# A state-space layer's gelu and its split issued per chunk inside the chunk loop, with the two scratch sets exchanging slots

## The chip, the cores and the metric

One core of one Trainium2 chip runs the whole program. The metric is the device time of one execution in microseconds (us), median of three runs. The engines are TensorE (PE, matmuls; its weight loads are PEld), VectorE (DVE), ScalarE (ACT), GpSimd (POOL) and SyncE (SP, which issues the DMAs). Each works through its own queue in order and waits on semaphores.

## The reference, cut to what matters

The network has two blocks in float32 over 256 tokens and 1024 channels. The first block runs four layers (short convolution, S5 state space, RWKV-7, short convolution), each ended by a gated projection and a layer norm. The second block runs over tokens and a context. The change sits in the state-space layer:

```python
u, z = jnp.split(x @ w_in, 2, axis=-1)
...
states = lax.associative_scan(_ssm_combine, (a_seq, bu), axis=1)[1]
y = jnp.einsum("blgp,ghp->blgh", states, c_mat).real + d_skip.astype(f32).reshape(SSM_GROUPS, SSM_GROUP) * ug
y = jax.nn.gelu(y.reshape(bsz, seqlen, D_INNER).astype(x.dtype))
y = y * jax.nn.sigmoid(y @ w_glu + b_glu)
return (y * jax.nn.silu(z)) @ w_out
```

## The kernel before

Activations lie as 8 chunks of 128 channels by 256 tokens. A large matmul takes three passes: weight and activation are each split into a rounded part (`hi`) and the rest (`lo`), and hi·hi, hi·lo and lo·hi are summed. So a 1024x128 weight tile is 24 matmuls of 128x256, and costs one DMA (L605), one ACT copy (`whi`, L606) and one DVE subtraction (`wlo`, L607), issued up to four tiles ahead. `split` does the same to an activation: an ACT copy and a DVE subtraction.

The state-space layer (`ssm`, L968) runs its 8 chunks through the generator `group(c)`, two at a time (`par`). A chunk computes cosines and sines of its angles (`phases`: two sines on ACT, which need ACT's sine table), projects (PE into `ps_ca`, `ps_cb`; ACT copies to `w`), rotates (DVE multiplies and adds, 128x1024 and 128x512), scans (8 DVE scans), rotates back, multiplies by C on PE (`ps_st`) and adds the skip (DVE, writes `y[:, c]`). Its scratch is one of two sets of two slots, `ssm_m`: the even chunks' set lies in slots 6 and 7, the odd chunks' in slots 0 and 1. A slot is a fixed place; a new tile in it waits until the last reader of the old one is done. `ys`, the split gelu, is made in slots 0 and 1, the odd set's.

After the loop, for all 8 chunks: gelu on ACT, then the split. Then the GLU matmul (8 tiles, 192 matmuls), whose results go through tanh on ACT and two products on DVE into `g` (split again), and the output matmul over `g`.

Two more things share the engines. A *context* stream (the second block's context, its first feed-forward: `squares`, `tc`, `h`, `td`, `d`) begins when `ssm` sets its stage after the chunk loop; from then on a planner (`weave`) alternates the two streams in program order by modelled times, taking the context's steps where the first block's stream is modelled as waiting, and a scheduler orders each engine's queue from that program. And a side chain (`junk`, L1384, with 512 KB loads from `in_ada`) is dealt out in between, except while the chunk loop holds it back.

Of the kernel before, what the change touches and what calls it, by code (L numbers as in the profile page):

```python
# [13 lines left out]
AF = mybir.ActivationFunctionType  # L14
# [6 lines left out]
NCH = D // 128  # L21
# [3 lines left out]
RAW = ("ssm_in",)  # L25
# [417 lines left out]
class Net:  # L443
# [491 lines left out]
    def phases(self, c, q_, make):  # L935


        A, V = self.A, self.V
        tsh, _, rho, f2 = self.pre[:4]
        if q_ not in self.sets:  # L940
            self.sets[q_] = tuple(self.slot(k, [2048], f"ssm_m{k}") for k in ((6, 7), (0, 1))[q_])
        a, b = self.sets[q_]
        m1, m2, w = (t.rearrange("p (i q t) -> p i q t", i=4, q=2) for t in (a[:, :1024], a[:, 1024:], b[:, :1024]))
        co, si = (b[:, 1024 + 512 * k:1536 + 512 * k].rearrange("p (i t) -> p i t", i=4) for k in range(2))
        v, kk = (a[:, 1024 + 512 * k:1536 + 512 * k].rearrange("p (i t) -> p i t", i=4) for k in range(2))
        if make:
            for i in range(4):
                self.tc.keep_in_program_order(A.activation(out=v[:, i], in_=tsh, func=AF.Identity, scale=f2[:, 4 * c + i:4 * c + i + 1]))
            A.activation(out=kk, in_=v, func=AF.Identity, bias=self.fixed[MAGIC])
            V.scalar_tensor_tensor(out=v, in0=kk, scalar=MAGIC, in1=v, op0=ALU.subtract, op1=ALU.subtract)  # L950
            self.act(si, v, AF.Sin, scale=-TWO_PI)
            A.activation(out=v, in_=v, func=AF.Abs)
            self.act(co, v, AF.Sin, scale=-TWO_PI, bias=self.fixed[1.5707963])
        return m1, m2, w, co, si
# [7 lines left out]
    def ssm(self, X):  # L962
        nc = self.nc
        x, xs = X
        V, A, T = self.V, self.A, self.T
        N = S // 2
        tt = lambda o, a, b, op: V.tensor_tensor(out=o, in0=a, in1=b, op=op)
        MUL, ADD, SUB = ALU.mult, ALU.add, ALU.subtract  # L968
        tsh, t11, rho, f2, bT, gm, ca, cm = self.pre
        full = lambda i, n: self.slot(i, [NCH, S], n)  # L970
        u, sz = full(8, "u"), full(9, "sz")

        def take(m, ps):
            if m < NCH:
                A.activation(out=u[:, m], in_=ps, func=AF.Copy)
            else:
                self.act(sz[:, m - NCH], ps, AF.Silu)


        came = []  # L980

        def project():
            for t in tiles:
                yield from self.linear("ssm_in", xs or x, take, tiles=(t,))
                came.append(t)

        tiles = [0, 1, 2, 3] + [t for c in range(4) for t in (NCH + c, 4 + c)] + [NCH + c for c in range(4, 8)]

        y = full(10, "y")
        cn = self.slot(3, [2, 32, 32], "cn")
        for r, cc in ((0, ca), (1, cm)):
            A.activation(out=cn[:, r], in_=cc[:, 1], func=AF.Copy, scale=-1.0)
        free = list(range(2))
        halves = lambda t: t.rearrange("p (t r) -> p r t", r=2)
        two = lambda t: t.rearrange("p (q t) -> p q t", q=2)
        lanes = [slice(32 * i, 32 * i + 32) for i in range(4)]

        def group(c):  # L1000
            q_ = free.pop(0)
            m1, m2, w, co, si = self.phases(c, q_, c > 1)
            while c not in came:
                yield Until(self.now() + 0.3)
            uc = two(self.tmp("ta"))
            A.activation(out=uc, in_=halves(u[:, c]), func=AF.Copy)
            both = lambda t: t.unsqueeze(2).to_broadcast([128, t.shape[1], 2, N])
            yield 2.0
            ps = [self.ps(("ca", "cb")[i % 2])[:, :S] for i in range(4)]
            for q in range(2):  # L1010
                for r in range(2):
                    for i, l in enumerate(lanes):
                        T.matmul(two(ps[i])[:, q], lhsT=bT[1 - r][l, q, c], rhs=uc[l, r], start=r == 0, stop=r == 1, share=4)
            for i in range(4):
                A.activation(out=w[:, i], in_=two(ps[i]), func=AF.Copy)
            tt(m1, w, both(co), MUL)
            tt(m2, w, both(si), MUL)
            tt(w[:, :, 0], m1[:, :, 0], m2[:, :, 1], ADD)
            tt(w[:, :, 1], m2[:, :, 0], m1[:, :, 1], SUB)
            for i in range(4):  # L1020
                for q in range(2):
                    x_ = w[:, i, q]
                    V.tensor_tensor_scan(out=x_, data0=rho[:, 4 * c + i:4 * c + i + 1].to_broadcast([128, N]), data1=x_, initial=0.0, op0=MUL, op1=ADD)
            tt(m1, w, both(co), MUL)
            tt(m2, w, both(si), MUL)
            yield 4.0
            yp = two(self.ps("st")[:, :S])
            for i in range(4):
                T.matmul(yp[lanes[i], 0], lhsT=gm[:, c, lanes[i]], rhs=uc[:, 0], start=True, stop=False, share=4)
            for r, cc in ((0, ca), (1, cm)):  # L1030
                n = N - 1 + r
                for k in range(4):
                    for i in range(4):
                        j = 4 * c + i
                        l_, m_ = ((cc[:, 0, j], m1[:, i, 0]), (cc[:, 0, j], m2[:, i, 1]), (cc[:, 1, j], m2[:, i, 0]), (cn[:, r, j], m1[:, i, 1]))[k]
                        T.matmul(yp[lanes[i], r, N - n:], lhsT=l_, rhs=m_[:, :n], start=r == 1 and k == 0, stop=k == 3, share=4)
            free.append(q_)
            V.scalar_tensor_tensor(out=halves(y[:, c]), in0=halves(u[:, c]), scalar=self.p("ssm_d", c), in1=yp, op0=MUL, op1=ADD)

        self.fine = FINE & 1  # L1040
        self.hold += 1
        yield from self.par((group(c) for c in range(NCH)), 2, project())
        self.fine = False
        self.hold -= 1
        self.stage = "ssm"
        yield 1.0
        raw = "ssm_glu" in RAW
        ys = y if raw else self.pair(0, 1, "ys")
        for c in range(NCH):
            self.tc.keep_in_program_order(self.act(y[:, c], y[:, c], AF.Gelu_apprx_tanh))  # L1050
            if not raw:
                self.split(y[:, c], ys[0][:, c], ys[1][:, c])
        yield 4.0
        g = self.operand("ssm_out", (2, 3), "g")
        hb = self.few.tile([128, NCH], F32, name="hb")
        V.tensor_scalar(out=hb, in0=self.p("b_glu", n=NCH), scalar1=0.5, scalar2=None, op0=MUL)

        def take_g(m, ps):
            th = self.tmp("ta")
            self.act(th, ps, AF.Tanh, scale=0.5, bias=hb[:, m:m + 1])  # L1060
            V.scalar_tensor_tensor(out=th, in0=th, scalar=1.0, in1=y[:, m], op0=ADD, op1=MUL)
            self.put(g, m, th, lambda o: V.scalar_tensor_tensor(out=o, in0=th, scalar=0.5, in1=sz[:, m], op0=MUL, op1=MUL))

        yield from self.linear("ssm_glu", ys, take_g)
        yield 1.5
        return (yield from self.finish(x, g, "ssm_out", "ple_gate1"))

# [906 lines left out]
```

## Time and profile before

| | us |
|---|---|
| median of 3 runs | 2878.42 (2876.4 to 2881.57) |
| profiled execution | 2878.2 |
| its span, first to last instruction | 2876.3 |
| PE busy in it | 2738.9 (95%) |
| DVE, ACT busy | 2130.2 (74%), 1596.7 (56%) |

The profiled execution is 0.2 us from the median and spends 1.9 us outside its span. PE is busy nearly throughout, so the places to look at are the few stretches in which it is not.

### The profile page before, as it was taken

The numbers are of one execution on the slowest core, as the hardware profiler recorded it, in microseconds if no ns is written. First come the engines' busy times: TensorE is split into PE (matmuls) and PEld (weight loads), VectorE is DVE, ScalarE is ACT, GpSimd is POOL, SyncE is SP. The second block draws the span as 40 slices with busy tenths as digits, with TensorE's granted clock in tenths as the row PEclk, the third lists the DMA queues.
The fourth block names the chain that finished last, engine by engine and source line by source line (L and its number), as shares of the span: only waits on it lengthen the run. The fifth ranks groups of instructions, "written<-read, shape, count | busy, mean of one in ns | idle before, by whom it ended". The sixth has DMA issues, their size and how long they took to land.

```text
span 2876.3 us, 58509 instructions
## 1 busy us (share of the span) xinstructions
PE 2738.9 (95%) x23798; PEld 2587.5 (90%) x23798; DVE 2130.2 (74%) x3951; ACT 1596.7 (56%) x2946; POOL 13.0 (0%) x40
## 2 busy tenths in 40 slices
PE   8978799899999999999999999999999999999999
PEld 8967699778998998998999968999999999996999
DVE  8867777666688788898889887777854556676654
ACT  6455555866655465877666766545422234466443
POOL 0000000000000000000000000000000000000000
PEclk9989799999999999999999999999999999999999
DMA  7743355201486665666575644666544433322554
GB/s 273 244 158 111 107 169 176 82 17 41 159 263 226 221 200 176 211 215 202 182 231 186 201 134 150 209 219 208 176 140 133 132 112 109 94 91 62 160 183 140
DMA packets 132749, 467.51 MB, mean 163 GB/s; under 512 B 14720, under 2 KB 19072, under 8 KB 131840
## 3 DMA queue, kind: packets, MB, share of 16 engines
q1 hardware_dynamic: 132480, 463.78, 50.3%
q8 instruction: 187, 3.06, 0.4%
q14 instruction: 82, 0.67, 0.1%
HBM read 462.67 MB, written 1.05 MB: 161 GB/s over the span
## 4 chain that ended last, share of the span: by engine, by line
PE 68%; DVE 13%; DMA 9%; ACT 6%; issue 4%; SPq 0%; DVEq 0%; ACTq 0%
PE ps_mm L436 58%; DMA w<-in_ada_dram 6%; PE ps_ca L436 5%; DVE wlo L607 4%; PE ps_cb L436 2%; DVE junk L1384 2%; ACT whi L606 2%; DVE ssm_m L406 2%; PE ps_st L436 2%; DVE tc L406 1%; PE ps_cb L440 1%; DMA w<-in_ab_in_dram 1%; ACT rw_b L406 1%; ACT L406 1%; DMA w<-in_ffn_in_dram 1%
## 5 line engine op out<-in xcount | busy, mean ns | idle before, releaser
L606 ACT ACTIVATE whi<-w 128x1024 fp32r<-128x1024 f32 (+1 forms) x687 | 716.0, 1043 | 738.1 <-PE ps_mm L436 476.0
L607 DVE TENSOR_TENSOR wlo<-w,whi 128x1024 fp32r<-128x1024 f32 (+1 forms) x687 | 826.0, 1204 | 249.7 <-ACT whi L606 247.0
L436 PE MATMUL ps_mm<-h_hi,whi 128*128 128x256 f32 x3024 | 871.4, 290 | 16.8 <-ACT h_hi L406 12.9
L436 PE MATMUL ps_mm<-h_hi,wlo 128*128 128x256 f32 x3024 | 857.8, 285 | 6.0 <-DVE wlo L607 5.8
L436 PE MATMUL ps_mm<-h_lo,whi 128*128 128x256 f32 x3024 | 855.7, 284 | 1.1 <-DVE h_lo L406 1.0
L436 PEld LDWEIGHTS ps_mm<-h_hi,whi 128*128 128x128 f32 x3024 | 571.9, 190 | 27.2 <-ACT h_hi L406 16.4
L436 PEld LDWEIGHTS ps_mm<-h_lo,whi 128*128 128x128 f32 x3024 | 575.2, 190 | 6.0 <-DVE h_lo L406 2.8
L436 PEld LDWEIGHTS ps_mm<-h_hi,wlo 128*128 128x128 f32 x3024 | 572.8, 190 | 8.5 <-DVE wlo L607 7.8
L1384 DVE SCALAR_TENSOR_TENSOR junk<-w,cond 128x1024 bf16<-128x1024 f32 x288 | 351.7, 1221 | 149.9 <-DMA w<-in_ada_dram 148.8
L436 PE MATMUL ps_mm<-d_hi,whi 128*128 128x256 f32 x1232 | 355.5, 289 | 3.6 <-DVE ctx L406 2.7
L436 PE MATMUL ps_mm<-d_hi,wlo 128*128 128x256 f32 x1232 | 349.6, 284 | 0.6 <-DVE wlo L607 0.6
L436 PE MATMUL ps_mm<-d_lo,whi 128*128 128x256 f32 x1232 | 349.6, 284 | 0.4 <-DVE d_lo L406 0.4
L436 PEld LDWEIGHTS ps_mm<-d_hi,whi 128*128 128x128 f32 x1232 | 232.1, 188 | 8.0 <-issue 5.4
L436 PEld LDWEIGHTS ps_mm<-d_lo,whi 128*128 128x128 f32 x1232 | 233.3, 189 | 3.4 <-issue 1.2
L436 PEld LDWEIGHTS ps_mm<-d_hi,wlo 128*128 128x128 f32 x1232 | 232.6, 189 | 1.6 <-DVE wlo L607 0.8
L406 DVE TENSOR_TENSOR td<-td,ps_mm 128x256 f32<-128x256 f32 x154 | 64.4, 418 | 71.8 <-PE ps_mm L436 70.6
L406 ACT ACTIVATE d_hi<-td 128x256 fp32r<-128x256 f32 x154 | 63.1, 410 | 90.5 <-DVE td L406 89.7
L406 ACT ACT_TABLE_LOAD x80 | 102.6, 1283 | 2.1 <-PEq L1965 0.7
L436 PE MATMUL ps_mm<-x_hi,whi 128*128 128x256 f32 x256 | 73.9, 289 | 10.7 <-ACT whi L606 10.7
L406 ACT ACTIVATE tc<-tc 128x256 f32<-128x256 f32 x182 | 75.0, 412 | 5.2 <-DVE tc L406 2.4
L436 PE MATMUL ps_mm<-xs_hi,whi 128*128 128x256 f32 x256 | 73.3, 287 | 4.8 <-ACT xs_hi L406 4.6
L406 ACT ACTIVATE td<-ps_mm 128x256 f32<-128x256 f32 x154 | 57.4, 374 | 32.7 <-PE ps_mm L436 32.2
(466 smaller groups left out, 5233.8 us busy)
## 6 DMA issues: line engine op xcount, KB each, us to landing
w<-in_ffn_in_dram SPq DMA_DIRECT2D x268, 512.0 KB, 4.0
w<-in_ada_dram SPq DMA_DIRECT2D x168, 512.0 KB, 4.3
w<-in_ffn_out_dram SPq DMA_DIRECT2D x96, 512.0 KB, 4.0
w<-in_conv_in_dram SPq DMA_DIRECT2D x64, 512.0 KB, 4.7
w<-in_ffn_out_dram SPq DMA_DIRECT2D x48, 384.0 KB, 3.1
w<-in_ab_in_dram SPq DMA_DIRECT2D x34, 512.0 KB, 4.2
w<-in_ple_gate_dram SPq DMA_DIRECT2D x32, 512.0 KB, 4.3
w<-in_conv_out_dram SPq DMA_DIRECT2D x16, 512.0 KB, 4.8
```

What stands on the lines that cost most here:

```text
L406: return f(**kw)
L436: self.t.matmul(out, lhsT=lhsT, rhs=rhs, start=start, stop=stop)
L440: self.t.transpose(out, in_, ident)
L606: nc.scalar.activation(out=hi[:, :n], in_=w[:, :n], func=AF.Copy)
L607: nc.vector.tensor_tensor(out=lo[:, :n], in0=w[:, :n], in1=hi[:, :n].bitcast(F32), op=ALU.subtract)
L1384: nc.vector.scalar_tensor_tensor(out=self.junk, in0=w, scalar=1.0, in1=cb[:, s], op0=ALU.mult, op1=ALU.mult, accum_out=m[:, t, s:s + 1])
```

## The change

`gelu` and `split` of a chunk move into `group`, behind the line that writes `y[:, c]`. Nothing is issued for the first six chunks; when the seventh is summed, `ys` is made and all seven are done in one go, and the eighth follows when it is summed. The two scratch sets exchange slots: the even chunks now use slots 0 and 1, which `ys` takes over, so it waits for chunk 6 and no more for chunk 7. The loop behind the chunk loop goes.

```diff
-            self.sets[q_] = tuple(self.slot(k, [2048], f"ssm_m{k}") for k in ((6, 7), (0, 1))[q_])
+            self.sets[q_] = tuple(self.slot(k, [2048], f"ssm_m{k}") for k in ((0, 1), (6, 7))[q_])
...
         free = list(range(2))
+        summed, gated, ys = [], set(), []
...
             V.scalar_tensor_tensor(out=halves(y[:, c]), in0=halves(u[:, c]), scalar=self.p("ssm_d", c), in1=yp, op0=MUL, op1=ADD)
+            summed.append(c)
+
+            if len(summed) >= NCH - 1:
+                if not ys:
+                    ys.extend(self.pair(0, 1, "ys"))
+                for k in [k for k in summed if k not in gated]:
+                    gated.add(k)
+                    self.tc.keep_in_program_order(self.act(y[:, k], y[:, k], AF.Gelu_apprx_tanh))
+                    self.split(y[:, k], ys[0][:, k], ys[1][:, k])
...
-        raw = "ssm_glu" in RAW
-        ys = y if raw else self.pair(0, 1, "ys")
-        for c in range(NCH):
-            self.tc.keep_in_program_order(self.act(y[:, c], y[:, c], AF.Gelu_apprx_tanh))
-            if not raw:
-                self.split(y[:, c], ys[0][:, c], ys[1][:, c])
-        yield 4.0
+        yield 1.5
...
-        yield from self.linear("ssm_glu", ys, take_g)
+        yield from self.linear("ssm_glu", tuple(ys), take_g)
```

The orders of the engines show what moves. On ACT, at the end of the chunk loop, before (`sz` is the last silu of the layer, `td` the context's silu; `ACT_TABLE_LOAD` switches ACT's function table):

```order
L406 ACTIVATE sz<-ps_mm 128x256
L406 ACTIVATE squares<-ctx 128x256 x8
L397 ACT_TABLE_LOAD
L406 ACTIVATE tc<-ps_mm,fixed_66 128x256
L406 ACTIVATE tc<-tc 128x256 x2
L406 ACTIVATE h_hi<-tc,mod 128x256 x8
L406 ACT_TABLE_LOAD
L406 ACTIVATE y<-y 128x256
L406 ACT_TABLE_LOAD
L406 ACTIVATE td<-ps_mm 128x256
L406 ACTIVATE ys_hi<-y 128x256
L406 ACT_TABLE_LOAD
```

On ACT there now, from the sixth of the eight gelus on; ahead of these rows stand `sz`, one table load and five pairs of `y` and `ys_hi`:

```order
L406 ACTIVATE y<-y 128x256
L406 ACTIVATE ys_hi<-y 128x256
L406 ACTIVATE y<-y 128x256
L406 ACTIVATE ys_hi<-y 128x256
L406 ACTIVATE squares<-ctx 128x256 x3
L406 ACTIVATE y<-y 128x256
L406 ACTIVATE squares<-ctx 128x256
L406 ACTIVATE ys_hi<-y 128x256
L406 ACTIVATE squares<-ctx 128x256 x4
L406 ACTIVATE ta<-ps_mm,hb 128x256
```

The context's norm (`tc`, `h_hi`) has moved from ahead of the first gelu to behind the last GLU tanh (`ta`), and three of the four table loads have left this place.

On DVE, in the last two chunks (tiles 2093 and 2094 are the even set, 2104 and 2105 the odd one), before:

```order
L607 TENSOR_TENSOR wlo<-w,whi 128x1024
L406 TENSOR_TENSOR ssm_m_2094<-ssm_m_2093 128x4x128 x2
L406 SCALAR_TENSOR_TENSOR ssm_m_2094<-rho,ssm_m_2094 128x128 x8
L406 TENSOR_TENSOR ssm_m_2104<-ssm_m_2105 128x1024
L406 TENSOR_TENSOR ssm_m_2093<-ssm_m_2094 128x1024 x2
L406 TENSOR_TENSOR ssm_m_2104<-ssm_m_2105 128x1024
L607 TENSOR_TENSOR wlo<-w,whi 128x1024
L406 TENSOR_TENSOR ssm_m_2105<-ssm_m_2104 128x4x128 x2
L406 SCALAR_TENSOR_TENSOR ssm_m_2105<-rho,ssm_m_2105 128x128 x8
L406 SCALAR_TENSOR_TENSOR y<-u,pr,ps_st 128x2x128
L406 TENSOR_TENSOR ssm_m_2104<-ssm_m_2105 128x1024 x2
L406 TENSOR_TENSOR squares<-squares 128x256 x6
```

And now:

```order
L607 TENSOR_TENSOR wlo<-w,whi 128x1024
L406 TENSOR_TENSOR ssm_m_2093<-ssm_m_2094 128x1024 x2
L406 TENSOR_TENSOR ssm_m_2094<-ssm_m_2093 128x4x128 x2
L406 SCALAR_TENSOR_TENSOR ssm_m_2094<-rho,ssm_m_2094 128x128 x8
L406 TENSOR_TENSOR ssm_m_2104<-ssm_m_2105 128x1024
L406 TENSOR_TENSOR ssm_m_2093<-ssm_m_2094 128x1024 x2
L406 TENSOR_TENSOR ssm_m_2104<-ssm_m_2105 128x1024
L406 TENSOR_TENSOR ssm_m_2105<-ssm_m_2104 128x4x128 x2
L406 SCALAR_TENSOR_TENSOR ssm_m_2105<-rho,ssm_m_2105 128x128 x8
L406 SCALAR_TENSOR_TENSOR y<-u,pr,ps_st 128x2x128
L406 TENSOR_TENSOR ssm_m_2104<-ssm_m_2105 128x1024 x2
L406 TENSOR_TENSOR ys_lo<-y,ys_hi 128x256 x7
```

Two `wlo` have left the run of the last rotations and scans; all four of the GLU's first weight tiles are now split ahead of it, where before stood two `junk` and, in between, the four `wlo` of one context tile and three GLU tiles. Seven `ys_lo` follow the last rotation where the context's squares were summed.

On PE, at the end of chunk 7, before and now:

```order
L436 MATMUL ps_st<-ssm_m_2104,cn 32x128 x4
L436 MATMUL ps_mm<-squares,cs_base 128x256 x2
L436 MATMUL ps_mm<-h_hi,whi 128x256
L436 MATMUL ps_mm<-h_lo,whi 128x256
L436 MATMUL ps_mm<-h_hi,wlo 128x256
```

```order
L436 MATMUL ps_st<-ssm_m_2104,cn 32x128 x4
L436 MATMUL ps_mm<-ys_lo,whi 128x256
L436 MATMUL ps_mm<-ys_hi,wlo 128x256
L436 MATMUL ps_mm<-ys_hi,whi 128x256
L436 MATMUL ps_mm<-ys_lo,whi 128x256
```

The GLU's matmuls now come straight behind chunk 7's, where 24 context matmuls (one weight tile) stood. Three matmuls over `ys_hi` even stand ahead of chunk 7's last group. Further on in PE's order, 48 context matmuls between the GLU and the output matmul are gone (the two sums of `squares` stand there now); in the layer norm that ends the layer, 48 context matmuls stand between the sums for the mean and for the variance, and before there were 72; in the next layer's norm, 96 stand behind the variance's sum, and before 22. By then both programs have issued nearly the same amount of context work. From there on the planner's choices differ in detail in the whole rest of the program, with the same instructions.

## Rows read from the trace of the kernel before

**Rows 1.** The page's summary: span, busy times, PE and its clock in 40 slices.
```profile
span 2876.3 us, 58509 instructions
...
PE   8978799899999999999999999999999999999999
...
PEclk9989799999999999999999999999999999999999
```

**Rows 2.** Stretches: us, busy us (count) of PE, PEld, DVE, ACT, POOL; clock, DMA share, GB/s.
```profile
291.50:308.30 16.80, 8.62 (x145) 5.92 (x145) 15.93 (x29) 4.23 (x10) 3.82 (x8) 0.70 0.22 76
308.30:327.30 19.00, 12.41 (x41) 9.42 (x41) 10.19 (x23) 12.86 (x24) 0.63 (x2) 0.59 0.10 30
327.30:330.00 2.70, 2.70 (x13) 2.70 (x14) 1.71 (x5) 2.60 (x8) 0.00 (x0) 0.53 0.59 191
340.00:350.00 10.00, 10.00 (x86) 10.00 (x85) 8.33 (x15) 5.58 (x11) 0.00 (x0) 1.00 0.72 213
...
425.00:450.00 25.00, 20.26 (x154) 19.84 (x153) 24.66 (x62) 17.13 (x34) 0.00 (x0) 0.93 0.36 121
...
880.00:890.00 10.00, 5.40 (x28) 5.08 (x27) 9.80 (x24) 8.19 (x20) 0.00 (x0) 0.66 0.50 162
```

**Rows 3.** Chain that ended last, pieces between 268 and 330 us.
```profile
272.95 3.99 DMA w<-in_ada_dram
...
278.29 3.40 DMA w<-in_ssm_glu_dram
...
288.04 1.14 DVE wlo L607
289.18 8.27 DVE ssm_m L406 x14
297.44 1.14 DVE wlo L607
298.58 3.75 DVE ssm_m L406 x10
302.33 0.37 DVE y L406
302.70 2.28 DVE ssm_m L406 x2
...
305.03 3.21 PE ps_st L436 x56
308.23 1.65 PE ps_mm L436 x4
```

**Rows 4.** The same chain asked for up to 420 us, its longest piece.
```profile
327.29 83.63 PE ps_mm L436 x684
```

**Rows 5.** ACT in order of time: start, us, operation, [idle before, releaser].
```profile
281.70 1.06 ACT L606 ACTIVATE whi<-w 128x1024 fp32r<-128x1024 f32 x1 [0.18 <-DMA w<-in_ssm_glu_dram]
...
291.52 0.38 ACT L406 ACTIVATE sz<-ps_mm 128x256 f32<-128x256 f32 x1 [2.88 <-PE ps_mm L436]
299.49 2.56 ACT L406 ACTIVATE squares<-ctx 128x256 f32<-128x256 f32 x8 [7.59 <-PE ps_st L436]
...
320.98 1.28 ACT L406 ACT_TABLE_LOAD   x1
322.27 0.38 ACT L406 ACTIVATE td<-ps_mm 128x256 f32<-128x256 f32 x1
...
326.61 0.40 ACT L406 ACTIVATE y<-y 128x256 f32<-128x256 f32 x1
327.04 0.42 ACT L406 ACTIVATE ys_hi<-y 128x256 fp32r<-128x256 f32 x1
327.36 0.40 ACT L406 ACTIVATE y<-y 128x256 f32<-128x256 f32 x1
```

**Rows 6.** PE's first matmul behind the GLU and DVE's last `g_lo`, in order of time.
```profile
350.11 0.28 PE L436 MATMUL ps_mm<-h_hi,whi 128*128 128x256 f32 x1
...
355.30 0.42 DVE L406 TENSOR_TENSOR g_lo<-ta,g_hi 128x256 fp32r<-128x256 f32 x1
```

## Prediction

> **What bounds the kernel now.** I read the page's summary first: PE is busy 2738.9 of 2876.3 us, and the slice row shows where it is not [rows 1]. Slices are 71.9 us; the third to fifth, 144 to 360 us, hold 7, 8 and 7 tenths, and the fifth also has the lowest clock, 0.7. The state-space layer lies there, so I asked for its stretches next [rows 2]. From 340 us on PE is full at clock 1.00. From 291.5 to 308.3 us DVE is full (15.93 of 16.80) and PE half idle: the last two chunks rotate and scan on DVE. From 308.3 to 327.3 us no engine is full: PE holds 12.41 of 19.00 us, at a mean clock of 0.59. A stretch without a full engine is a chain of short steps, so the chain comes third [rows 3]: DVE until 304.98, chunk 7's 56 matmuls until 308.23, the context's sum of squares on PE until 309.88; then, up to 327.29, the context's norm, its eight `h`, the gelu and the splits on ACT and DVE, one behind the other; and then 684 PE matmuls in 83.63 us without a break [rows 4]. The GLU's matmuls could have run once chunk 7 was summed, just after 308.23. They did not because the first gelu stands behind the whole of the context's norm in ACT's order, and because the silu `td` between the first gelu and its split costs table loads to and fro [rows 5].
>
> **The change, part by part.**
>
> *The hole after the last chunk.* PE is to start the GLU right behind chunk 7's matmuls. Between 308.23 and 327.29 it now spends 19.06 us. Of the work in there 41 matmuls count [rows 2]: 4 for the squares' sum [rows 3], 24 for a context tile (the order), so 13 of the GLU. The 37 large ones cost 83.63 / 684 = 0.122 us each when PE runs freely [rows 4], 4.5 us; the 4 cost 1.65 us here [rows 3], at a low clock, and I take 1.0. All of this is still to be done, later, at full rate. So 19.06 - 5.5 = 13.6 us are lost there now. That is the main term.
>
> *Will the gelus be ready?* ACT's last silu ends at 291.9, and ACT then idles 7.59 us until chunk 6's matmuls free a slot, at 299.49 [rows 5]. In the new order the table load and the first gelu fit in that gap. The first `ys_hi` must wait for chunk 6's matmuls, as `squares` did, because `ys` takes the even set's slots: also 299.5, since chunk 6 loses one `wlo` and gains a wait of the same size (below). A pair of gelu and copy takes 0.75 us (326.61 to 327.36) [rows 5], so seven pairs end at 299.5 + 5.3 = 304.8, and 3 squares (0.32 each, from 2.56 for 8) at 305.8. Seven `ys_lo` on DVE behind the last rotation need about 2.9 us at 0.42 each, as long as `g_lo` [rows 6], until 306.7. All of it is done before chunk 7's matmuls end (307.0, below), so these 14 ACT and 7 DVE instructions cost nothing; without the cover of the rotations they would cost 5.3 us. What is late next is chunk 7 itself: sum 0.4, gelu 0.4, a square 0.3, copy 0.4, the rest of the squares' sums in front of `ys_lo` 0.5, `ys_lo` 0.4: 2.4 us. Of the first GLU tile, 18 matmuls don't need it: 2.2 us at full clock, 3.8 at half. I take 0 (bounds 0 and 2.4). Three `ys_hi` matmuls stand ahead of chunk 7's in PE's order, which is harmless, because `ys_hi` of chunk 2 (about 301.7) comes before chunk 7's last rotation.
>
> *The chunks' end on DVE.* Two `wlo` leave the chain: 2 x 1.14 = 2.3 us [rows 3]. Against it, the four GLU tiles are now loaded and split in front of the last rotations, and in SP's order the second and the fourth load wait for a `wlo`. The first load comes in place of the first `in_ada` load and its `wlo` in place of the first `junk`; the second lands as the second `in_ada` load did, at 272.95 + 3.99 = 276.9 [rows 3]; its copy and `wlo` end at 279.3; the fourth load lands 3.4 to 4.0 us later [rows 3], say 283.1, against 281.7 for the load awaited there now [rows 5]. In ACT's order the sine comes ahead of that wait, so I take 1.1 us, with bounds 0 and 3.4. Net: 1.2 us earlier (from 1.1 later to 2.3 earlier): the last rotation ends at 303.8 instead of 304.98, chunk 7's matmuls at 307.0.
>
> *TensorE's clock.* Now PE starts its free run at the lower of its two levels (1.2 and 2.4 GHz): 13 matmuls take 2.70 us at a mean clock of 0.53, 0.21 us each, before it has 1.00 [rows 2]. That it had been working on 41 matmuls before did not spare it that, so by this row the GLU's new start costs nothing more. Around PE's restart in the next layer's norm the mean is 0.66 over 10 us, which makes 6.8 us at the lower level [rows 2]; if the GLU had as much, 4.1 us more than now, it would lose 4.1 x (1 - 0.122 / 0.21) = 1.7. The new start follows a stretch with PE half idle at 0.70 [rows 2], so I take 0.7, nearer to the first row (bounds 0 and 1.7). The Trainium skill (TensorE: Matmul & The Clock Gate, "HAM oscillation — how this bites in real kernels") speaks against the change: idle gaps of PE bring the throttle back, and the next burst then starts cold. By that rule the sum would lose the whole 1.7 and the time would be 2865.6; by the row it would be 2863.9.
>
> *Behind the GLU.* The last tile's tanh, products and split end 5.6 us after its matmuls (350.11 to 355.72) [rows 6]. Before, 48 context matmuls (5.8 us) covered this; now the squares' sum (1.0) and the 21 matmuls of the first output tile that don't need the last chunk (2.6) do. A wait of up to 2.0 us opens; I take 1.5.
>
> *The norms.* In this layer's norm 24 matmuls fewer fill PE between the two sums: 0 to 2.9 us lost, I take 1.0, since 4.7 of 25 us are idle there already [rows 2]. In the next layer's norm 74 more stand behind the variance's sum, where PE is idle 4.6 of 10 us at 0.66 [rows 2]: a gain of 0 to 6.0 (the idle time and some of the clock's loss); I take 2.0, since DVE, full there with 9.80 of 10, must split their weights too.
>
> *Sum.* 13.6 + 1.2 - 0.7 - 1.5 - 1.0 + 2.0 = 13.6 us. The profiled execution took 2878.2 us (span and 1.9 around it), and the median is 0.2 above it: 2878.2 - 13.6 = 2864.6. The rest of the program, in which PE is nearly full [rows 1], is only dealt out anew; that can be worth a few us either way, about 2 by the size of the single terms above, and I add nothing for it.
>
> **The rivals.** A change within 0.2% (5.8 us) cannot be told from none here.
>
> *Half the gain.* The weight loads ahead of the rotations cost all their 3.4 us, the last chunk's gelu and split 2.4 more, and DVE, 8.33 of 10 busy in the GLU as it was [rows 2], falls behind with squares and `junk` added, another 2: 3.4 - 1.1 = 2.3, plus 2.4, plus 2, on top of 2864.6, is 2871. For it: DVE's load. Against it: four tiles are split ahead, and DVE's work for a tile (two products, `g_lo`, `wlo`, 2.5 us) fits in 24 x 0.122 = 2.9.
>
> *Given back later.* The planner's new choices lose about 10 us in the remaining 2500, through waits like those of the norms: 2875. For it: the order differs to the end. Against it: the moved context work sits where PE is idle.
>
> *More.* The next norm's hole is filled whole and DVE gains its 2.3: 2864.6 - 4.0 - 1.1 - 2 = 2857.5.
>
> *The clock stays low: slower.* PE's context matmuls used to run just ahead of the GLU. Without them the GLU could run at 1.2 GHz throughout: 0.21 - 0.122 = 0.088 us more for each matmul. From 13.6 / 0.088 = 155 matmuls on the gain is gone; through GLU and output (384) it costs 34, giving 2898. Against it: in every stretch of free running read here PE came to 1.00 within 7 us, and then kept it [rows 2].
>
> *It doesn't do what it says.* If `ys_hi` had to wait for chunk 7, as before the slots changed places, the split would start at 308.2 and PE would wait some 2 us for the first pair, then 0.75 us for each: about 2867, still faster, since the context's norm is out of the way.
>
> **How the numbers follow.** Forecast near 2864.6, from 2858 to 2869: 0.58 (with the last rival's outcome). More, 2854 to 2858: 0.10. Half, 2869 to 2872.7: 0.16. Given back, 2872.7 to 2884: 0.12. Slower, above 2884: 0.04. Faster 0.84, same 0.12, slower 0.04. The range runs from 2855, where every bound is good, to 2875, into the cases that give the gain back; about 0.06 lies below and 0.12 above.
>
> **What would show it.** Chunk 7's last matmul ends near 307 and the GLU's run begins there, not at 327.3; one table load stands between the last silu and the first gelu; the first `ys_hi` starts when chunk 6's matmuls end, near 299; the context's norm falls into the output matmul, with PE full; PE's break behind the GLU stays under 2 us. It is wrong if DVE ends its last rotation later than 304.98, if the clock stays at half beyond 5 us of the GLU, or if PE's idle time after 420 us grows by more than 5 us.

## The result, and the profile after

| | before | after |
|---|---|---|
| median | 2879.99 us, 4 runs | 2866.74 us, 4 runs (2862.89 to 2868.72) |
| profiled execution, its span | 2878.2, 2876.3 us | 2865.13, 2863.3 us |
| PE busy | 2738.9 us | 2732.0 us |

The ratio is 0.9949, with a 95% interval of 0.9929 to 0.9969: faster by 0.5%, 2.1 us above the forecast of 2864.6 and inside its range.

The page's summary (before: [rows 1]): the fifth slice, which held the hole, has gone from 7 to 8 tenths of PE and its clock from 0.7 to 0.8.

```profile
span 2863.3 us, 58502 instructions
...
PE   8978899899999999999999999999999999999999
...
PEclk9989899999999999999999999999999999999999
```

The chain that ended last, pieces between 268 and 330 us of the changed kernel (before: [rows 3]; start, us, what):

```profile
273.76 5.16 DMA w<-in_ssm_glu_dram
...
281.28 3.50 DMA w<-in_ssm_glu_dram
...
288.11 2.37 DVE ssm_m L406 x2
...
303.11 2.28 DVE ssm_m L406 x2
...
305.44 3.20 PE ps_st L436 x56
308.64 21.39 PE ps_mm L436 x170
```

Chunk 7's last matmul ends at 308.64 and the GLU runs on from there without a break: the 19.06 us between 308.23 and 327.29 are gone. The last rotation, however, ends at 305.39 and not at 303.8: two waits for weight loads stand ahead of it.

Stretches of the changed kernel (columns as in [rows 2]):

```profile
200.00:330.00 130.00, 111.63 (x1244) 95.08 (x1243) 100.19 (x173) 67.89 (x152) 5.40 (x10) 0.91 0.35 113
291.50:308.64 17.14, 10.93 (x154) 7.47 (x152) 16.20 (x33) 6.84 (x16) 3.65 (x8) 0.70 0.11 32
308.64:310.64 2.00, 2.00 (x10) 2.00 (x11) 1.45 (x4) 1.94 (x7) 0.79 (x2) 0.55 0.67 207
310.64:332.31 21.67, 21.67 (x182) 21.67 (x181) 19.34 (x37) 13.46 (x26) 0.96 (x1) 1.00 0.60 198
330.00:410.00 80.00, 77.49 (x625) 75.99 (x624) 64.74 (x126) 54.42 (x97) 0.00 (x0) 1.00 0.52 165
403.30:428.30 25.00, 19.87 (x143) 19.46 (x142) 24.08 (x60) 15.94 (x33) 0.00 (x0) 0.86 0.42 139
835.00:885.00 50.00, 45.68 (x352) 44.74 (x351) 43.87 (x84) 30.23 (x56) 0.10 (x1) 0.93 0.63 207
```

The same stretches of the kernel before, where [rows 2] has none (the last one lies 15 us later, as the program does there):

```profile
200.00:330.00 130.00, 104.69 (x1118) 85.28 (x1118) 96.34 (x168) 66.11 (x148) 5.40 (x10) 0.84 0.30 98
330.00:410.00 80.00, 80.00 (x667) 79.88 (x667) 58.22 (x94) 44.99 (x75) 0.00 (x0) 1.00 0.58 180
850.00:900.00 50.00, 43.35 (x330) 42.11 (x329) 44.49 (x88) 29.31 (x55) 0.10 (x1) 0.93 0.66 213
```

By 330 us PE has done 126 matmuls more than before (1244 - 1118), 15.4 us at 0.122. In the next 80 us it loses 42 of them again (667 - 625, 5.1 us): 2.5 us because it idles, most of the rest because some matmuls take longer than 0.122 us, namely the sums of `squares` (4 in 0.86 us) and those of the layer's norm (10 in 2.7 us), which comes some 20 us earlier and so begins inside the stretch. The norm's idle time lies behind 410 us in both kernels.

ACT at the end of the chunk loop (before: [rows 5]):

```profile
294.13 1.28 ACT L406 ACT_TABLE_LOAD   x1
295.43 0.42 ACT L406 ACTIVATE y<-y 128x256 f32<-128x256 f32 x1
300.79 0.42 ACT L406 ACTIVATE ys_hi<-y 128x256 fp32r<-128x256 f32 x1 [4.95 <-PE ps_st L436]
...
305.32 0.42 ACT L406 ACTIVATE ys_hi<-y 128x256 fp32r<-128x256 f32 x1
308.70 1.03 ACT L406 ACTIVATE squares<-ctx 128x256 f32<-128x256 f32 x3 [2.97 <-PE ps_st L436]
```

One table load stands between the last silu and the first gelu, the first `ys_hi` starts when chunk 6's matmuls end (300.79, 1.3 us later than expected), and ACT has finished seven pairs 2.97 us before chunk 7 is there.

The chain behind the GLU, and around PE's idle time up to 410 us:

```profile
332.31 0.86 PE ps_st L436 x4
333.18 2.99 PE ps_mm L436 x25
...
336.17 8.77 PE ps_mm L436 x70
...
353.32 1.15 DVE wlo L607
...
354.52 4.99 DMA w<-in_ple_gate_dram
...
361.00 11.10 PE ps_mm L436 x89
```

Behind the GLU there is no break. But the context's norm (`tc`, `h_hi`, `h_lo`) holds up the weights' copies on ACT and subtractions on DVE, so that PE waits 0.7 us for a `whi` and 0.7 for a `wlo`, just before 352.00 and 353.04. The buffer that the next `wlo` frees is reloaded late, and PE waits once more, for 1.1 us just before 361.00, for an ACT step (`pp`) that stands in ACT's queue behind this load's `whi`. These three waits are its 2.5 us of idle time.

### The profile page after: what moved, and what is told of

Read it like the earlier page. It is cut to its first block, busy times and chain, and to the rows that moved or that the text cites. A ratio compares the mean times of both kernels' runs of the same rounds, so it can differ in the third digit from the quotient of the medians.

```text
span 2863.3 us, 58502 instructions
## 1 busy us (share of the span) xinstructions
PE 2732.0 (95%) x23798; PEld 2583.9 (90%) x23798; DVE 2127.2 (74%) x3951; ACT 1593.4 (56%) x2946; POOL 13.0 (0%) x40
## 4 chain that ended last, share of the span: by engine, by line
PE 69%; DVE 12%; DMA 9%; ACT 7%; issue 3%; SPq 0%; ACTq 0%; DVEq 0%
PE ps_mm L436 59%; DMA w<-in_ada_dram 5%; PE ps_ca L436 4%; DVE wlo L607 3%; PE ps_cb L436 2%; DVE junk L1388 2%; ACT whi L606 2%; DVE ssm_m L406 2%; PE ps_st L436 2%; DVE tc L406 1%; DMA w<-in_ffn_in_dram 1%; ACT rw_b L406 1%; PE ps_cb L440 1%; ACT tc L406 1%; ACT L406 1%
## 5 line engine op out<-in xcount | busy, mean ns | idle before, releaser
L406 DVE TENSOR_TENSOR td<-td,ps_mm 128x256 f32<-128x256 f32 x154 | 64.3, 418 | 66.4 <-PE ps_mm L436 65.0
L406 ACT ACTIVATE d_hi<-td 128x256 fp32r<-128x256 f32 x154 | 63.1, 410 | 86.9 <-DVE td L406 86.4
L406 ACT ACTIVATE tc<-tc 128x256 f32<-128x256 f32 x182 | 75.0, 412 | 4.3 <-DVE tc L406 1.4
L406 ACT ACTIVATE td<-ps_mm 128x256 f32<-128x256 f32 x154 | 57.2, 374 | 34.3 <-PE ps_mm L436 33.3
```

What stands on the lines that cost most here:

```text
L406: return f(**kw)
```

## The experiments

"Ratio" is the time over that of the kernel before, run beside it on the same chip, with its 95% interval. One and the same program started its GLU 2 us later in another execution (308.64 above, 310.70 in the sixth experiment), so small differences are read between neighbouring rows of one execution, or from the ratio.

**1 and 2. The two halves of the change apart.**

The first is the kernel before with the slots exchanged and nothing else:

```diff
-            self.sets[q_] = tuple(self.slot(k, [2048], f"ssm_m{k}") for k in ((6, 7), (0, 1))[q_])
+            self.sets[q_] = tuple(self.slot(k, [2048], f"ssm_m{k}") for k in ((0, 1), (6, 7))[q_])
```

> The kernel before with nothing but the two sets' slots exchanged; the gelus keep their place in the code, behind the chunks and behind the start of the context's stream. Theory: the slots decide who may go first. The context's squares take slot 6, which now belongs to the odd set, so they must wait for chunk 7's matmuls (about 308.2 us in place of 299.5), and the gelus, free of the norm, stand right behind the eight squares in ScalarE's order. So the GLU starts behind squares (2.6 us), a table load (1.3) and one pair (0.75), near 313, and its first tile is paced by the pairs of 0.75 us until about 319: some 7 to 8 us behind the changed kernel, in all near 2874 (2870 to 2878). Rival: the place of the gelus in the code is what counts, the swap alone gains nothing and makes the context's norm 3 us later: 2880 to 2883, with the GLU's free run beginning near 327 or later.

Ratio 1.0013 (1.0002 to 1.0023). From the chain that ended last:

```profile
308.83 3.25 PE ps_st L436 x56
...
312.16 0.73 ACT squares L406 x2
...
317.99 9.48 PE ps_mm L436 x72
...
329.86 0.52 ACT h_hi L406 x2
```

The theory was right about the place (squares behind chunk 7, the GLU's run from 318) and wrong about the time, 2887.14 us in place of some 2874. The run is not free: after 72 matmuls the context's norm (`h_hi`) comes in between, now inside the GLU, as this stretch shows:

```profile
330.00:410.00 80.00, 75.01 (x601) 74.18 (x601) 60.59 (x101) 43.93 (x75) 0.00 (x0) 0.96 0.58 181
```

Where the kernel before does 667 matmuls, this one does 601. PE idles 4.99 us, all of it before 350, in its longest wait 3.62 us for a `wlo` on DVE, and its granted clock is 0.66 from 340 to 350.

The second is the changed kernel with the old slots:

```diff
-            self.sets[q_] = tuple(self.slot(k, [2048], f"ssm_m{k}") for k in ((0, 1), (6, 7))[q_])
+            self.sets[q_] = tuple(self.slot(k, [2048], f"ssm_m{k}") for k in ((6, 7), (0, 1))[q_])
...
-            if len(summed) >= NCH - 1:
+            if len(summed) >= NCH:
```

> The changed kernel with the two sets back in their old slots (and the gelus, for that reason, written behind the sum of all eight chunks). Theory: without the swap the split must wait for chunk 7's matmuls while the context's squares may go at 299.5, so the norm's logarithm and exponentials fall between the gelus again, with a table load each way: the GLU's free run begins near 327 as before, and the time is that of the kernel before within 3 us, 2877 to 2881. Rival (the case that the prediction called doesn't do what it says): with the gelus ahead of the context's norm in the code, the split only starts 3 us later and the time is near 2867 to 2870.

Ratio 1.0003 (0.9992 to 1.0015). The chain between chunk 7 and the GLU's run; `ACT L406` of 1.28 us is a table load:

```profile
308.76 1.28 ACT L406
310.06 0.42 ACT y L406
310.50 1.28 ACT L406
311.79 0.47 ACT tc L406
...
312.59 1.28 ACT L406
...
318.73 6.45 PE ps_mm L436 x36
```

The norm's steps do fall between the gelus, with table loads to and fro, as the theory had it, but the run starts at 318.7 and not at 327. So each half alone starts the GLU's run some 9 us earlier than before (327.29) and gains nothing in the end; the time expected of the second came about for another reason than the one given. With the slots alone the lead is gone at once: by 410 us PE has done 20 matmuls fewer than before. Where the rest went is seen from the first `xs_hi` matmul of the fourth layer on, which starts at 885.09, 883.41 and 876.83 us in the kernel before and in these two. PE's matmuls up to there, and from there to 1200 us, in the kernel before:

```profile
0.00:885.09 885.09, 796.07 (x8354) 732.54 (x8354) 653.69 (x1283) 521.90 (x1093) 8.80 (x32) 0.95 0.47 152
885.09:1200.00 314.91, 304.31 (x2420) 299.62 (x2420) 260.19 (x437) 190.58 (x315) 1.46 (x6) 0.98 0.65 209
```

behind that point with the slots alone:

```profile
883.41:1200.00 316.59, 297.82 (x2334) 291.22 (x2333) 261.68 (x436) 185.46 (x300) 1.45 (x6) 0.97 0.64 210
```

and with the order alone:

```profile
876.83:1200.00 323.17, 305.16 (x2417) 298.89 (x2416) 270.68 (x454) 195.24 (x318) 1.45 (x6) 0.98 0.66 212
```

The same work is done at that point in all three (8354 matmuls, 8354 and 8355), 1.7 us earlier with the slots alone and 8.3 with the order alone. But the latter then needs 323.17 us for what takes 314.91 before: the whole 8.3 are given back by 1200 us, in a stretch in which the edit itself moves nothing and the planner merely deals the work out anew. With the slots alone 86 matmuls are missing there. From this point to the span's end it is 1991.2 us before, 2004.2 and 2000.2 here, and 1993.3 in the changed kernel, which has 24 matmuls (2.9 us) of the context still to do at its 870.00. The changed kernel's rest is thus as good as before, and that of each half worse by 13 and 9 us in these executions (by the ratios, which give 3.7 and 0.9 us more in the whole, by 5 and 9).

**3. The GLU's second to fourth weight tiles split later.** Their copies are issued behind chunk 7's cosine, their subtractions behind its first rotation:

```diff
-            self.act(co, v, AF.Sin, scale=-TWO_PI, bias=self.fixed[1.5707963])
+            self.pa = self.act(co, v, AF.Sin, scale=-TWO_PI, bias=self.fixed[1.5707963])
...
-            tt(m2, w, both(si), MUL)
+            self.pv = tt(m2, w, both(si), MUL)
...
+        after = lambda ins: self.tc.issue_after(ins.ins) if ins and name == "ssm_glu" and 0 < i < 4 else ExitStack()
-        nc.scalar.activation(out=hi[:, :n], in_=w[:, :n], func=AF.Copy)
+        with after(self.pa): nc.scalar.activation(out=hi[:, :n], in_=w[:, :n], func=AF.Copy)
```

and the same with `self.pv` around the subtraction.

> The changed kernel, in which the copies and subtractions of the GLU's second to fourth weight tiles are issued behind chunk 7's cosine on ScalarE and behind chunk 7's first rotation on VectorE; TensorE's order is the same but for three pairs in the GLU. Theory: the loads' wait and the copies behind it hold up the last two chunks' rotations (VectorE idle 5.7, 0.5, 1.9 and 1.0 us between 274 and 288 us); without them chunk 6's first rotation starts near 284.5 in place of 288.1, one subtraction comes back in among the rotations (1.1), the last rotation ends near 303 in place of 305.4 and the GLU starts near 306.3 in place of 308.6; the end of the program moves by as much: 2864.4, 2.3 us below the changed kernel. Rival: the three subtractions (3.4 us) come to lie in the GLU, where VectorE then feeds it late, and the gain is spent there: GLU's end unchanged at 332, time 2866 to 2868.

Ratio 0.9921 (0.9904 to 0.9939), median 2860.11. Its chain:

```profile
283.49 2.37 DVE ssm_m L406 x2
...
301.82 3.20 PE ps_st L436 x56
305.03 23.39 PE ps_mm L436 x189
```

No load is left in the chain between 272 and 301. The first rotation starts at 283.49 (288.11 with the change alone), and the GLU takes no longer than it did (23.39 us against 23.67, 308.64 to 332.31): three subtractions more do not slow it. The gain, 3.6 us at the GLU's start (5.7 beside experiment 6) where 2.3 were expected, is there at the span's end (2859.0 against 2863.3 and, in experiment 6, 2862.9). The wait for weight loads in front of the last rotations did cost about this much.

**4. The context's stream let in behind the GLU.**

```diff
-        self.stage = "ssm"
         yield 1.0
...
         yield from self.linear("ssm_glu", tuple(ys), take_g)
+        self.stage = "ssm"
```

> The changed kernel, in which the context's stream is let in behind the GLU's matmuls in place of behind the chunks; the two products of the conditioning then run among the last chunks as they did before, and three weight subtractions with them, the norm's parts come a few instructions later in the output matmul, and the program's later part keeps its order. Theory: TensorE's idle 2.5 us near 359 us come from the context's norm holding up the weights' subtractions on VectorE; the norm is no shorter, so the hole stays or moves, and the whole changes by less than 2 us: 2865 to 2869. Rival: the norm's earlier place is what costs, and with the norm behind the GLU the hole closes: 2864, TensorE full from 330 to 410.

Ratio 0.9944 (0.9928 to 0.9959). Its stretch:

```profile
330.00:410.00 80.00, 78.76 (x637) 77.35 (x636) 65.12 (x127) 54.74 (x97) 0.00 (x0) 1.00 0.51 167
```

PE's idle time there is 1.24 us in place of 2.51: half of what the rival expected. The two waits that the norm causes directly have shrunk from 1.4 to 0.2 us; the waits for `pp` remain, 1.0 us. The whole is the changed kernel's, as the theory said. The GLU starts at 310.94, where experiment 6 starts it at 310.70; whether the conditioning's products, back among the last chunks, cost more there than the weight tiles that they replace is not shown, since two executions of one program differ by more.

**5. Both.** Experiment 3, with the stage and the release of the conditioning (`self.hold -= 1`) moved behind the GLU.

> The third experiment's later splits and the fourth's later context in one kernel (the conditioning's products stay behind the GLU too, so that none of them comes among the last chunks). Theory: the two are separate places, so both gains stay: the GLU starts near 305 us as in the third experiment, and TensorE's idle time between 330 and 410 (4.2 us there) falls to the fourth's 1.2: 3 us below the third experiment, near 2857, ratio to before 0.991. Rival: with three subtractions more in the GLU VectorE is late for the norm, which then holds the next weights as before: 2860, no better than the third.

Ratio 0.9917 (0.9900 to 0.9933), median 2858.16; PE idles 2.88 us between 330 and 410 where experiment 3 idled 4.20.

The idle time falls by 1.32 us, as it did in experiment 4 (by 1.27), but the 3 us expected are not there: half of what is left, 1.5 us, is a wait for the context's `td` that experiment 3 has too. The total cannot tell this version from experiment 3. Both beat the kernel before by 0.8%, and the changed kernel by 0.2% to 0.3%, though their intervals reach into its own.

**6 to 8. The changed kernel again, and two other deals of its later part.**

```diff
-GAPS = (6.5, 10., 12., 12.)
+GAPS = (6.5, 9.5, 12., 12.)
```

and 10.5 in experiment 8.

> The changed kernel itself once more, beside the other variants on the same chip. Theory: its ratio to before lies inside the first measurement's interval, 0.993 to 0.997; the third experiment (0.992) is then a gain of some 0.25% over it, and the fourth (0.994) none. Rival: the first measurement was low by chance, and 0.992 is its own value too.

> The changed kernel with the planner's spacing of the conditioning's steps in the fourth layer and later 9.5 in place of 10: every engine's order is the same until about 790 us, and dealt out anew behind it, with the same instructions in all. It measures by how much such a deal moves the end. Theory (from the first two experiments, in which the TensorE work up to 700 us was done 6 us earlier or 2 later than before, and the rest took 6 to 9 us more): another deal is worth several us by itself, so this ends 3 to 8 us from the changed kernel, on either side. Rival, as the prediction put it: about 2 us either way, 2865 to 2869.

> The same with a spacing of 10.5: the order is the same until about 740 us. Theory: 3 to 8 us from the changed kernel, on either side, and not the mirror image of the shorter spacing. Rival: within 2 us of the changed kernel.

Ratios 0.9940 (0.9924 to 0.9955), 0.9978 (0.9967 to 0.9989) and 0.9935 (0.9916 to 0.9954). The longer spacing changes nothing that can be measured, the shorter one gives back two thirds of the gain, 11 us by the medians (2865.37 and 2876.53). Its place: two stretches of the changed kernel in experiment 6,

```profile
1960.00:2000.00 40.00, 40.00 (x333) 39.90 (x332) 31.73 (x59) 23.92 (x42) 0.00 (x0) 1.00 0.58 183
2000.00:2040.00 40.00, 36.81 (x283) 35.66 (x282) 33.87 (x65) 21.92 (x39) 0.00 (x0) 0.96 0.48 152
```

and of experiment 7:

```profile
1960.00:2000.00 40.00, 33.06 (x260) 32.54 (x260) 33.67 (x63) 18.46 (x33) 0.00 (x0) 0.94 0.51 164
2000.00:2040.00 40.00, 37.22 (x265) 35.65 (x265) 33.88 (x62) 24.12 (x37) 0.00 (x0) 0.89 0.60 192
```

91 matmuls fewer in 80 us, 11 us (of which 21 had been gained up to 1960, so 8 us remain at 2040). In experiment 7 PE waits 6.78 us there, up to 1997.19, for a `wlo` that stands on DVE behind the steps of a norm over the context (`tc`, `h_lo`). In experiment 6 a norm of the other stream lies there, and PE waits 2.73 us, up to 2004.22. Which norm lies where, and how much of it other work covers, thus differs from deal to deal.

**9. The early split taken away.** All `ys_hi` are issued behind the gelu of chunk 7:

```diff
-            if len(summed) >= NCH - 1:
+            if len(summed) >= NCH:
...
-                    self.split(y[:, k], ys[0][:, k], ys[1][:, k])
+                for k in range(NCH): self.tc.keep_in_program_order(A.activation(out=ys[0][:, k], in_=y[:, k], func=AF.Copy)); V.tensor_tensor(out=ys[1][:, k], in0=y[:, k], in1=ys[0][:, k].bitcast(F32), op=SUB)
```

> The changed kernel, in which all eight splits of the gelus are issued behind the gelu of chunk 7 on ScalarE (the seven gelus themselves stay early); the program's later part keeps its order. It takes from the change what the prediction's last rival took from it: the early split, but not the context's norm out of the way. Theory: behind chunk 7's last matmul come its sum (0.4), its gelu (0.4), the first copy and subtraction (0.8), and then the pairs follow each other as fast as TensorE uses them (0.31 and 0.35 against 0.37 us for three matmuls), so about 2 us are lost: from chunk 7's last matmul to the GLU's last 25.5 us in place of 23.7 (332.31 - 308.64), time 2867 to 2868 beside 2865.4. Rival: TensorE starts the GLU at its lower clock and so needs 0.6 us for three matmuls, and hides most of it: below 0.7 us, 2866.

Ratio 0.9948 (0.9933 to 0.9963). Its chain:

```profile
305.21 3.25 PE ps_st L436 x56
...
308.53 0.72 ACT squares L406 x2
...
309.56 0.32 ACT ys_hi L406
...
309.92 23.40 PE ps_mm L436 x192
333.32 0.86 PE ps_st L436 x4
```

From chunk 7's last matmul (308.46) to the GLU's last, 333.32, it takes 24.86 us, against 23.67: 1.2 us, between the two expectations, since PE's start waits 1.46 us and the rest follows as fast as PE asks. The total cannot show this.

## Why the prediction was right, point by point

*The hole after the last chunk* (13.6): right. The GLU begins in the same moment in which chunk 7 ends. Together with the terms of the chunks' end and of the clock 14.1 us were forecast up to the GLU, and by 330 us PE is 126 matmuls, 15.4 us, ahead. Most of this is the context's norm out of the way and not the early split: with the splits behind chunk 7 but no norm between them (experiment 9) the GLU's run starts 1.46 us behind chunk 7 and 1.2 us are lost, while with the norm's steps and their table loads in between (experiment 2) it starts 10.5 us behind it (308.26 to 318.73). What the seven early gelus alone are worth no run shows; they are early in experiment 9 too. Nor is it either half of the edit: with the slots alone the squares wait for chunk 7 and the norm then falls into the GLU, with the order alone the norm comes between the gelus. The number seven in the edit matters not at all: written with the condition at all eight chunks, the kernel has the same order of instructions on every engine. What the edit sets is who is written first, and which set's slots the split inherits.

*The gelus ready* (0): right, with 2.97 us to spare on ACT.

*The chunks' end on DVE* (1.2 earlier): mis-sized, the one term with the wrong sign. The last rotation ended at 305.39 (at 307.45 in experiment 6), 0.4 us later than before; the prediction named this as a sign that it is wrong. I had charged the second weight load 3.99 us, the time of the load in its place before; it took 5.16, and the fourth load 3.50 behind a `wlo` that was late for it. So the waits ate the 2.3 us gained. The bound (3.4) held, and experiment 3 shows that the loads are the cause: with the copies issued behind the phases the last rotation ends at 301.78.

*The clock* (-0.7, bounds 0 and 1.7): the better bound held. The GLU's first 2.00 us have a mean of 0.55, then 1.00: the lower level lasts no longer than before, where 2.70 us had 0.53 [rows 2]. The Trainium skill (TensorE: Matmul & The Clock Gate, "HAM oscillation — how this bites in real kernels") says that a burst behind idle gaps starts cold. The trace agrees that it starts at the lower level, but no longer than before, so that the 1.7 us that I had worked out with that rule were not lost.

*Behind the GLU* (-1.5): not lost. `g_lo` of the last tile was charged 5.6 us behind the matmuls, as before; PE goes on at 336.17, 3.86 behind 332.31, without a gap.

*The norms* (-1.0 and +2.0): both right in sign and size. In this layer's norm 143 matmuls run in 25 us for 154 before [rows 2], 1.3 us lost; around the next norm 352 in 50 us for 330, 2.7 gained.

*What was missing:* I expected the context's norm to fall into the output matmul "with PE full". It did fall there, but it delays a `whi`, a `wlo` and through these a reload of 4.99 us, and PE idles 2.5 us in three waits. This is a wait of the kind that I had charged to the next norm only.

*The rest* ("about 2" either way): the size was wrong, the sum not. 15.4 - 2.5 - 1.3 + 2.7 = 14.3 us against 13.0 in the span leaves 1.3 lost in all the rest. The point of equal work says where: up to the fourth layer's first `xs_hi` the changed kernel is 885.09 - 870.00 - 2.9 = 12.2 us ahead, and the program behind it adds the last 0.8. Nearly all of the gain is thus made up to there (by 410 us PE is 79 matmuls, 9.6 us, ahead) and not by the deal of the 2000 us that follow. That the whole came so near to the forecast (13.0 in the span for 13.6) is in part luck, however: a chunks' end 1.6 us worse than forecast and the 2.5 us that were missing were largely made up by the clock (0.7 better), the break behind the GLU (1.5) and the next norm (0.7). And experiments 1, 2 and 7 show that another deal of the same work can cost 5 to 13 us (in experiments 1 and 2 as far as one execution of each tells), and experiment 8 that it can be worth nothing. The rival "given back later" deserved more than its 0.12; that it did not come true here is no merit of the change. Why a given edit leads to a good or a bad deal was not settled. Of the other rivals, the clock that stays low did not come (1.00 from 310.64 on), and a split that has to wait for chunk 7 costs 1.2 us and not 2.4.

## What to carry to other kernels

Where two streams share the engines' queues, look at what stands ahead of the first instruction that PE waits for: here it was another stream's norm, and code order together with the buffer that the waiting step inherits removed it, neither of them alone. Then look at weight loads that stand in the queue ahead of a latency-bound chain, since moving only their splits gave about 4 us more in the span (2859.0 against 2863.3 and 2862.9). And where a planner deals out everything behind the edit anew, put a range of the size of its deals on the forecast (here up to 11 us between two spacings, nearly the edit's own 13), and judge the edit at a point where the same work is done.

## What the hardware showed that was not expected

Three loads of the same 512 KB took 5.16, 3.50 and 4.99 us in one execution of the changed kernel (from 273.76, 281.28 and 354.52 on). And PE came up to its higher level after 2 us of the GLU although it had been idle for a third of the 17 us ahead of it, at a mean clock of 0.70.
